# State of a chunked scan kept in the values tile, query products one half step earlier, and the last projections spread over more steps

## The chip, the cores and the metric

The kernel runs on one core of one Trainium2 chip. The metric is the device time of one execution in microseconds (us), the median over repeated runs; a profile of one execution shows when each engine worked. Engines are TensorE (PE in the profile), its weight load (PEld), VectorE (DVE), ScalarE (ACT), GpSimd (POOL) and SyncE (SP, which issues most transfers).

## The reference

One inference step of a two-layer hybrid encoder: 2048 new frames of one stream and 16 frames of each of 8 running streams, model width 1024. The first layer is a gated DeltaNet, the second an RWKV-7 time mixer with 16 heads of 64. The change is in the second layer only, whose recurrence is this (cut):

```
def mixer_b(h, x_prev, s0, mu, w_in, ...):
    ...
    rkvz = jnp.einsum('gbtd,dge->gbte', xs[:4], w_in.reshape(D, 4, W_B)).astype(f32)
    ...
    def step(S, inp):
        r_t, w_t, k_t, v_t, a_t, b_t = inp
        sa = jnp.einsum('bhvk,bhk->bhv', S, a_t)
        S = S * w_t[:, :, None, :] + sa[..., None] * b_t[:, :, None, :] + v_t[..., None] * k_t[:, :, None, :]
        return S, jnp.einsum('bhvk,bhk->bhv', S, r_t)
    ...
    S, o = lax.scan(step, s0.astype(f32), seq)
    ...
    y = o.astype(h.dtype) @ w_out
```

The final state S of the prompt stream is an output, and so are y and the states of the running streams.

## The kernel before

The first layer takes the first 2450 us. The second is done in six blocks of columns (frames): the first has two chunks of 64 frames and the running streams, the other five have six chunks each (384 columns). A block has eight head pairs q; a pair fills 128 partitions, 64 for each head. `b_steps` runs over the 48 combinations of block and pair as a pipeline of steps i. In step i the parts of several pairs run side by side: preparation of pair i, substitution of pair i-1 (`b_subst`: the triangular solve on VectorE, L842 and L844 in turn on the tiles sbt and TB, closed by the copy L847), inverse of pair i-2 (L1282 is its first product and reads T, which L1266 on GpSimd writes), scan of pair i-3 (`b_scan`), gate of pair i-4, output projection of two pairs every other step (L168, L169, L170), and the input projections of the next block (the stream `st`; L1060, L1061, L1062). A step has twelve rounds, and each part is a generator that is advanced a given number of times over the rounds.

The order in which this code emits matmuls is TensorE's order. The other engines' order is made by a list scheduler from due times, which come from the places of the consumers in TensorE's order.

A scan takes two half steps for each chunk c, usually one in each round. The tile XV[c] holds for each head the state in the head's own 64 partitions and the chunk's values in the others; R[q] holds the state of the pair in 128 partitions over all blocks. In the first half step TensorE forms px from XV[c] (L1380), ScalarE makes Sw, the state times the chunk's decay wc (L1382, from R), and then copies px over the state in XV[c] (L1383, L1384). In the second, TensorE forms the query product from R into po (L1387), pu from XV[c] (L1391) and the rest of po (L1396), and VectorE writes the next state twice: as two halves into XV[c+1] (L1393) and whole into R (L1394). po is one PSUM tile with one buffer; `b_centre` (L1455 to L1458, result OC) reads it when the scan is over. The gate (`b_gate`) turns OC on TensorE (L106), forms og in the tile bv (L1483, L1484) and splits it into oh (ScalarE) and ol (VectorE, L163) for the output projection; it also reads SZ, a kept projection result that comes by a transfer.

The projections come in units of six matmuls 128x384 (two for each of L1060, L1061, L1062), spread evenly over the rounds of a step: PACE = 17 units in a step, and LAST_PACE = 8 from step 40 on. At step 40 there are 57 units left.

Of the kernel before, what the change touches and what calls it, by code (L numbers as in the profile page):

```python
# [18 lines left out]
KT = 8  # L19
# [52 lines left out]
class _K:  # L72
# [856 lines left out]
    def b_steps(self, blocks, st):  # L929

        npair = len(blocks) * KT
        def at(i):
            return (blocks[i // KT], i % KT) if 0 <= i < npair else None
        self.b_load(*at(0))
        for i in range(npair + 6):
            parts = []
            if at(i):
                parts.append((self.b_prep(*at(i)), range(1, 13)))
            if at(i - 2):
                parts.append((self.b_inverse(*at(i - 2)), (1, 2, 3, 4, 5, 6, 7, 8, 10)))  # L940
            if at(i - 4):
                parts.append((self.b_gate(*at(i - 4)), (1, 2, 3, 6)))
            if at(i - 1):
                parts.append((self.b_subst(*at(i - 1)), range(1, 9)))
            if at(i - 3):
                b = at(i - 3)[0]
                parts.append((self.b_scan(*at(i - 3)), 2 * b["ncp"] + 6 * b["nsc"], 0.0, 1.0))
            j = i - 5
            if at(j) and j % 2 == 0:
                out = self.b_out(blocks[j // KT], (j % KT, j % KT + 1))  # L950
                if j < npair - 2:
                    parts.append((out, 8, 0.5, 1.0))
                else:
                    parts.append((chain(out, self.b_final(blocks[j // KT])), 21, 0.5, 1.0))
            if at(j) and j % KT == KT - 1 and j < npair - 1:
                parts.append((self.b_final(blocks[j // KT]), 13, 0.0, 1.0))
            m = PACE if i < npair - KT else LAST_PACE
            parts.append((islice(st, m), m, 0.0, 1.0))
            self.rounds(ROUNDS, parts)
            if at(i + 1):  # L960
                self.b_load(*at(i + 1))
        for p in range(KT):
            self.nc.sync.dma_start(self.io["o_pw"][p], self.R[p])
# [391 lines left out]
    def b_scan(self, b, q):  # L1355
# [16 lines left out]
                nc.sync.dma_start(SS[u], io["sw"][q][:, 4 * u:4 * u + 4])  # L1372
        for h in range(2):
            nc.gpsimd.tensor_copy(XV[HS[h], 0, h], self.R[q][HS[h]])
        for c in range(ncp):
            S = self.R[q]
            wc = wcs[:, c:c + 1]
            px = self.ps("r")
            for h in range(2):
                nc.tensor.matmul(px[HS[h], 0:64], lhsT=GM[:, c, h, 0:64], rhs=XV[:, c, h], start=True, stop=True, tile_position=(0, 64 * h))  # L1380
            Sw = self.mp.tile([P, 64], F32, name=self.nm("Sw"), tag="Sw", bufs=2)
            nc.scalar.activation(Sw, S, AF.Copy, scale=wc)  # L1382
            nc.scalar.copy(XV[HS[0], c, 0], px[HS[0], 0:64])  # L1383
            nc.scalar.copy(XV[HS[1], c, 1], px[HS[1], 0:64])  # L1384
            yield
            for h in range(2):
                nc.tensor.matmul(po[HS[1 - h], c * 64:(c + 1) * 64], lhsT=KR[HS[h], c, 1], rhs=S[HS[h]], start=True, stop=False,  # L1387
                                 tile_position=(64 * h, 64 - 64 * h))
            pu = self.ps("r")
            for h in range(2):  # L1390
                nc.tensor.matmul(pu[HS[h], 0:64], lhsT=TM[:, c, h], rhs=XV[:, c, h], start=True, stop=True, tile_position=(0, 64 * h))  # L1391
            for h in range(2 if c + 1 < ncp else 0):
                nc.vector.scalar_tensor_tensor(XV[HS[h], c + 1, h], pu[HS[h], 0:64], wc[HS[h]], Sw[HS[h]], op0=MUL, op1=ADD)  # L1393
            nc.vector.scalar_tensor_tensor(S, pu[:, 0:64], wc, Sw, op0=MUL, op1=ADD)  # L1394
            for h in range(2):
                nc.tensor.matmul(po[HS[1 - h], c * 64:(c + 1) * 64], lhsT=GM[:, c, h, 64:P], rhs=XV[:, c, h], start=False, stop=True, tile_position=(0, 64 - 64 * h))  # L1396
            yield
# [272 lines left out]
```

## Time and profile before

| | us |
|---|---|
| median of 3 runs (lowest, highest) | 4619.62 (4618.65, 4632.22) |
| the profiled execution's own time | 4624.97 |
| its span in the trace | 4623.2 |
| mean granted TensorE clock | 0.962 of full |
| busy: TensorE, VectorE, ScalarE, GpSimd | 4311.4, 3477.9, 2286.9, 1743.4 |

The span is what the trace covers from the first to the last instruction; 1.8 us of the execution's own time lie around it. Busy times are sums over the engine's instructions, so they say how full an engine is, and not which one ends a stage.

### The profile page before, as it was taken

What the parts mean: (1) busy time and instruction counts of PE and PEld (TensorE: products, weight loads), DVE (VectorE), ACT (ScalarE), POOL (GpSimd) and SP (SyncE); (2) the same over time, 40 slices, a digit from 0 to 9 for tenths busy, and PEclk for the clock granted to TensorE, in tenths of its full rate; (3) what the DMA queues carried; (4) which work ended last, traced back from release to release, by engine and by line L of the source; (5) the groups of instructions that cost most, each with busy time, mean ns of one, the idle gap of its engine ahead of it and who ended that gap; (6) DMA issues with size and microseconds to landing.
All of it is one profiled execution on the core that took longest, in us unless ns stands there. A gap on an engine that the chain in (4) does not pass through costs nothing. (4 is left out here: it accounts for less than half of the span.)

```text
span 4623.2 us, 104068 instructions
## 1 busy us (share of the span) xinstructions
PE 4311.4 (93%) x37093; PEld 3708.7 (80%) x37093; DVE 3477.9 (75%) x9203; ACT 2286.9 (49%) x6132; POOL 1743.4 (38%) x2507
## 2 busy tenths in 40 slices
PE   7999999999999999999987988999999999999996
PEld 6888788888888899999886767777878887887775
DVE  7888776676666766776677888877778778778874
ACT  5555454454344434434465565555555455445542
POOL 7666443322112211211204455545344434434441
PEclk9999999999999999999998989999999999999987
DMA  6666665556555676676555667756666665665542
GB/s 192 209 202 208 210 211 172 172 183 193 143 142 159 176 210 183 185 213 189 173 163 170 204 203 229 224 172 193 195 196 180 193 202 162 201 195 145 141 126 67
DMA packets 765670, 842.18 MB, mean 182 GB/s; under 512 B 263480, under 2 KB 497360, under 8 KB 765152
## 3 DMA queue, kind: packets, MB, share of 16 engines
q1 hardware_dynamic: 765152, 835.53, 60.2%
q8 instruction: 294, 4.82, 0.4%
q14 instruction: 224, 1.84, 0.1%
HBM read 632.73 MB, written 202.53 MB: 181 GB/s over the span
## 5 line engine op out<-in xcount | busy, mean ns | idle before, releaser
L451 PE MATMUL ps<-hh,whl 128*128 128x384 f32 (+1 forms) x1960 | 796.0, 406 | 10.7 <-ACT hh L162 9.4
L453 PE MATMUL ps<-hh,whl 128*128 128x384 f32 (+1 forms) x1960 | 712.5, 364 | 6.5 <-POOL whl L125 6.5
L452 PE MATMUL ps<-hl,whl 128*128 128x384 f32 (+1 forms) x1960 | 712.1, 363 | 1.7 <-DVE hl L163 1.5
L1060 PE MATMUL ps<-xh,whl 128*128 128x384 f32 (+1 forms) x1632 | 606.8, 372 | 33.6 <-ACT xh L162 20.4
L1061 PE MATMUL ps<-xl,whl 128*128 128x384 f32 (+1 forms) x1632 | 560.2, 343 | 18.3 <-POOL xl L163 8.9
L1062 PE MATMUL ps<-xh,whl 128*128 128x384 f32 (+1 forms) x1632 | 558.6, 342 | 8.6 <-DVE whl L125 8.3
L125 POOL TENSOR_TENSOR whl<-wraw,whl 128x256 fp32r<-128x256 f32 x454 | 374.3, 830 | 354.1 <-ACT whl L124 326.3
L571 DVE SCALAR_TENSOR_TENSOR cv<-pre,cw,cv 128x512 f32<-128x512 f32 (+3 forms) x576 | 376.4, 662 | 137.8 <-ACT cv L569 130.7
L451 PEld LDWEIGHTS ps<-hh,whl 128*128 128x128 f32 x1960 | 372.5, 190 | 63.0 <-issue 13.7
L168 PE MATMUL ps<-oh,whl 128*128 128x384 f32 (+2 forms) x1024 | 390.6, 381 | 26.7 <-DMA whl<-wd 14.2
L124 ACT CAST whl<-wraw 128x256 fp32r<-128x256 f32 x726 | 286.8, 402 | 250.8 <-DMA wraw<-in_w_b 70.6
L453 PEld LDWEIGHTS ps<-hh,whl 128*128 128x128 f32 x1960 | 371.9, 190 | 46.8 <-POOL whl L125 11.2
L452 PEld LDWEIGHTS ps<-hl,whl 128*128 128x128 f32 x1960 | 373.1, 190 | 34.6 <-DVE hl L163 5.2
L1060 PEld LDWEIGHTS ps<-xh,whl 128*128 128x128 f32 x1632 | 321.2, 197 | 76.5 <-ACT xh L162 26.5
L169 PE MATMUL ps<-ol,whl 128*128 128x384 f32 (+2 forms) x1024 | 367.2, 359 | 7.0 <-DVE ol L163 7.0
L842 DVE TENSOR_TENSOR sbt<-B,TB 48x15 f32<-48x15 f32 (+14 forms) x1320 | 350.0, 265 | 23.1 <-DMA B<-scr 2.3
L170 PE MATMUL ps<-oh,whl 128*128 128x384 f32 (+2 forms) x1024 | 364.6, 356 | 1.4 <-POOL whl L125 1.4
L844 DVE TENSOR_TENSOR TB<-TB,sbt 48x15 f32<-48x15 f32 (+14 forms) x1320 | 350.7, 266 | 19.8
L1061 PEld LDWEIGHTS ps<-xl,whl 128*128 128x128 f32 x1632 | 323.5, 198 | 30.0 <-DVE xl L163 15.5
L1062 PEld LDWEIGHTS ps<-xh,whl 128*128 128x128 f32 x1632 | 323.0, 198 | 16.0 <-DVE whl L125 15.3
L820 DVE TENSOR_TENSOR x<-x,ps 128x384 f32<-128x384 f32 (+1 forms) x320 | 191.0, 597 | 79.4 <-PE ps L170 79.1
L168 PEld LDWEIGHTS ps<-oh,whl 128*128 128x128 f32 x1024 | 197.6, 193 | 66.0 <-ACT oh L162 9.9
(349 smaller groups left out, 10249.7 us busy)
## 6 DMA issues: line engine op xcount, KB each, us to landing
whl<-wd SPq DMA_DIRECT2D x1582, 256.0 KB
wd<-whl SPq DMA_DIRECT2D x428, 256.0 KB
wraw<-in_w_a SPq DMA_DIRECT2D x288, 128.0 KB
wraw<-in_w_b SPq DMA_DIRECT2D x256, 128.0 KB
kvd<-kvo SPq DMA_DIRECT2D x160, 192.0 KB
xn<-x1d SPq DMA_DIRECT2D x80, 192.0 KB
wraw<-in_w_ao SPq DMA_DIRECT2D x96, 128.0 KB
xn<-in_x SPq DMA_DIRECT2D x32, 256.0 KB
```

Of the source, the lines that this page charges most:

```text
L125: (self.nc.gpsimd if tag == "o" else self.weng).tensor_tensor(w[:, 1], raw, w[:, 0].bitcast(F32), op=SUB)
L168: self.nc.tensor.matmul(out, lhsT=wh, rhs=hh, start=first and i == 0, stop=False)
L169: self.nc.tensor.matmul(out, lhsT=wh, rhs=hl, start=False, stop=False)
L170: self.nc.tensor.matmul(out, lhsT=wl, rhs=hh, start=False, stop=i == n - 1)
L451: nc.tensor.matmul(p, lhsT=wh[:, k % 2], rhs=hh, start=k == 0, stop=False)
L452: nc.tensor.matmul(p, lhsT=wh[:, k % 2], rhs=hl, start=False, stop=False)
L453: nc.tensor.matmul(p, lhsT=wl[:, k % 2], rhs=hh, start=False, stop=k == KT - 1)
L571: nc.vector.scalar_tensor_tensor(o, f(j), self.cw[:, ct, j:j + 1], o, op0=MUL, op1=ADD)
L844: nc.vector.tensor_tensor(T[:, j + 1:16, 0:j + 1], T[:, j + 1:16, 0:j + 1], o, op=SUB)
L1060: nc.tensor.matmul(o, lhsT=wh[:, i], rhs=xh, start=k == 0, stop=False)
L1061: nc.tensor.matmul(o, lhsT=wh[:, i], rhs=xl, start=False, stop=False)
L1062: nc.tensor.matmul(o, lhsT=wl[:, i], rhs=xh, start=False, stop=k == KT - 1)
```

## The change

There are three edits. First, in all chunks but a scan's last VectorE writes the new state only into XV[c+1]; R[q] is written once, after the last chunk, where it carries the state to the next block and to the output. ScalarE's Sw is therefore made from the two state halves in XV[c], as two operations on 64 partitions, ahead of the copies of px that overwrite them. Second, the query product reads the state from XV[c], and stands in the first half step ahead of px. Third, in the last four steps of the 48 and after them the pace of projections is 4 units a step in place of 8.

```
@@ b_steps
-            m = PACE if i < npair - KT else LAST_PACE
+            m = PACE if i < npair - KT else LAST_PACE if i < npair - 4 else LAST_PACE // 2
@@ b_scan
         for c in range(ncp):
-            S = self.R[q]
             wc = wcs[:, c:c + 1]
+            for h in range(2):
+                nc.tensor.matmul(po[HS[1 - h], c * 64:(c + 1) * 64], lhsT=KR[HS[h], c, 1], rhs=XV[HS[h], c, h], start=True, stop=False,
+                                 tile_position=(64 * h, 64 - 64 * h))
             px = self.ps("r")
...
-            nc.scalar.activation(Sw, S, AF.Copy, scale=wc)
-            nc.scalar.copy(XV[HS[0], c, 0], px[HS[0], 0:64])
-            nc.scalar.copy(XV[HS[1], c, 1], px[HS[1], 0:64])
+            for h in range(2):
+                nc.scalar.activation(Sw[HS[h]], XV[HS[h], c, h], AF.Copy, scale=wc[HS[h]])
+            for h in range(2):
+                nc.scalar.copy(XV[HS[h], c, h], px[HS[h], 0:64])
             yield
-            for h in range(2):
-                nc.tensor.matmul(po[HS[1 - h], c * 64:(c + 1) * 64], lhsT=KR[HS[h], c, 1], rhs=S[HS[h]], start=True, stop=False,
-                                 tile_position=(64 * h, 64 - 64 * h))
             pu = self.ps("r")
...
-            for h in range(2 if c + 1 < ncp else 0):
-                nc.vector.scalar_tensor_tensor(XV[HS[h], c + 1, h], pu[HS[h], 0:64], wc[HS[h]], Sw[HS[h]], op0=MUL, op1=ADD)
-            nc.vector.scalar_tensor_tensor(S, pu[:, 0:64], wc, Sw, op0=MUL, op1=ADD)
+            if c + 1 < ncp:
+                for h in range(2):
+                    nc.vector.scalar_tensor_tensor(XV[HS[h], c + 1, h], pu[HS[h], 0:64], wc[HS[h]], Sw[HS[h]], op0=MUL, op1=ADD)
+            else:
+                nc.vector.scalar_tensor_tensor(self.R[q], pu[:, 0:64], wc, Sw, op0=MUL, op1=ADD)
```

In the changed code the lines have other numbers: L1387 becomes L1379, L1380 becomes L1383, L1391 becomes L1392, L1396 becomes L1399, the writes of XV and R become L1395 and L1397, Sw L1386 and the copies L1388, the centre L1458 to L1461, and the gate's two products L1486 and L1487. The 57 units left at step 40 went out as eight in each of steps 40 to 46 and one in step 47; now steps 40 to 43 have eight each, steps 44 to 49 four each and step 50 one. There are 256 chunks in 48 scans, so R was written 256 times and is written 48 times; Sw took 256 operations on ScalarE and takes 512. The number of matmuls is the same.

TensorE, one chunk of a scan in step 21, before (matmuls of other parts stand between the two half steps; ps_44548 is po, the other ps are px and pu):

```order
L1380 MATMUL ps_44809<-XV_43904,GM_42912 64x64 x2
...
L106 MATMUL ps_44848<-ident,OC_44448 64x64 x12
L1387 MATMUL ps_44548<-R_30368,KR_42575 64x64 x2
L1391 MATMUL ps_44875<-XV_43904,TM_43903 64x64 x2
L1396 MATMUL ps_44548<-XV_43904,GM_42912 64x64 x2
```

The same chunk now (po is ps_44566):

```order
L1379 MATMUL ps_44566<-XV_43924,KR_42590 64x64 x2
L1383 MATMUL ps_44829<-XV_43924,GM_42927 64x64 x2
...
L106 MATMUL ps_44869<-ident,OC_44466 64x64 x12
L1392 MATMUL ps_44894<-XV_43924,TM_43923 64x64 x2
L1399 MATMUL ps_44566<-XV_43924,GM_42927 64x64 x2
```

The query product moved from the start of the second half step to the start of the first, and reads XV.

VectorE, behind that same chunk's second half step, before (m is a small tile of the preparation, xt and xl belong to the inputs of the projections):

```order
L1191 TENSOR_SCALAR m_11116_44784<-m_11116_44784 128x6
L842 TENSOR_TENSOR sbt_44684<-B_44437,TB_44539 48x60
L1483 SCALAR_TENSOR_TENSOR bv_42031<-ps_44848,hp,bv_42031 128x384
L1393 SCALAR_TENSOR_TENSOR XV_43904<-ps_44875,wc_42560,Sw_44812 64x64 x2
L1484 SCALAR_TENSOR_TENSOR bv_42031<-bv_42031,hp,SZ_44531 128x384
L1394 SCALAR_TENSOR_TENSOR R_30368<-ps_44875,wc_42560,Sw_44812 128x64
L844 TENSOR_TENSOR TB_44539<-TB_44539,sbt_44684 48x10x6
L163 TENSOR_TENSOR xl_44720<-xt_44716,xh_44719 128x384
L163 TENSOR_TENSOR ol_44864<-bv_42031,oh_44863 128x384
```

And now:

```order
L844 TENSOR_TENSOR TB_44557<-TB_44557,sbt_44699 48x11x5
L163 TENSOR_TENSOR xl_44741<-xt_44737,xh_44740 128x384
L1395 SCALAR_TENSOR_TENSOR XV_43924<-ps_44894,wc_42575,Sw_44832 64x64 x2
L1486 SCALAR_TENSOR_TENSOR bv_42045<-ps_44869,hp,bv_42045 128x384
L842 TENSOR_TENSOR sbt_44702<-B_44457,TB_44557 48x60
L1487 SCALAR_TENSOR_TENSOR bv_42045<-bv_42045,hp,SZ_44549 128x384
L844 TENSOR_TENSOR TB_44557<-TB_44557,sbt_44702 48x10x6
```

The write of R is gone, and XV's pair moved ahead of the gate's first product and of one substitution operation.

VectorE, the end of the last substitution in step 48, before:

```order
L844 TENSOR_TENSOR TB_62224<-TB_62224,sbt_62415 48x4x12
L842 TENSOR_TENSOR sbt_62428<-B_62162,TB_62224 48x39
L844 TENSOR_TENSOR TB_62224<-TB_62224,sbt_62428 48x3x13
L1394 SCALAR_TENSOR_TENSOR R_30374<-ps_62521,wc_60675,Sw_62515 128x64
L842 TENSOR_TENSOR sbt_62431<-B_62162,TB_62224 48x28
L1455 TENSOR_REDUCE gn_62527<-ps_62233 128x6
L844 TENSOR_TENSOR TB_62224<-TB_62224,sbt_62431 48x2x14
L1456 TENSOR_SCALAR gn_62527<-gn_62527 128x6
L842 TENSOR_TENSOR sbt_62462<-B_62162,TB_62224 48x15
L1458 TENSOR_TENSOR OC_62528<-ps_62233,gn_62527 128x384
L844 TENSOR_TENSOR TB_62224<-TB_62224,sbt_62462 48x15
L847 COPY TB_62224<-TB_62224 48x256
```

And now:

```order
L844 TENSOR_TENSOR TB_62190<-TB_62190,sbt_62397 48x4x12
L842 TENSOR_TENSOR sbt_62417<-B_62117,TB_62190 48x39
L844 TENSOR_TENSOR TB_62190<-TB_62190,sbt_62417 48x3x13
L842 TENSOR_TENSOR sbt_62420<-B_62117,TB_62190 48x28
L844 TENSOR_TENSOR TB_62190<-TB_62190,sbt_62420 48x2x14
L842 TENSOR_TENSOR sbt_62454<-B_62117,TB_62190 48x15
L844 TENSOR_TENSOR TB_62190<-TB_62190,sbt_62454 48x15
L847 COPY TB_62190<-TB_62190 48x256
L1395 SCALAR_TENSOR_TENSOR XV_61680<-ps_62502,wc_60667,Sw_62476 64x64 x2
L1397 SCALAR_TENSOR_TENSOR R_30374<-ps_62519,wc_60667,Sw_62514 128x64
L1458 TENSOR_REDUCE gn_62525<-ps_62199 128x6
```

The scan's last two writes and the centre moved behind the substitution's closing copy; earlier in the same substitution a kept value's product (L1086) came in, since projection units now run in this step.

## Rows read from the trace of the kernel before

**Rows 1.** The page's first part: busy time of each engine, share of the span, instructions

```profile
PE 4311.4 (93%) x37093; PEld 3708.7 (80%) x37093; DVE 3477.9 (75%) x9203; ACT 2286.9 (49%) x6132; POOL 1743.4 (38%) x2507
```

**Rows 2.** Table of stretches: window, length, busy by engine (instructions), granted clock, DMA

```profile
2759.70:4169.60 1409.90, 1316.14 (x15421) 1120.41 (x15420) 1116.97 (x2929) 746.32 (x2021) 636.02 (x778) 0.96 0.66 195
...
4367.80:4402.90 35.10, 33.19 (x445) 27.58 (x444) 29.41 (x81) 18.56 (x54) 18.99 (x20) 0.85 0.47 132
4402.90:4445.10 42.20, 37.48 (x475) 31.97 (x475) 34.59 (x89) 15.56 (x47) 18.92 (x27) 0.92 0.69 209
4445.10:4476.60 31.50, 30.47 (x429) 25.05 (x428) 23.70 (x73) 15.14 (x46) 14.38 (x17) 0.84 0.32 86
4476.60:4513.00 36.40, 31.83 (x433) 25.11 (x432) 30.11 (x81) 14.82 (x46) 18.30 (x25) 0.91 0.34 87
4513.00:4536.90 23.90, 13.80 (x327) 11.32 (x326) 15.76 (x61) 11.49 (x38) 7.48 (x10) 0.88 0.17 35
4536.90:4562.20 25.30, 22.92 (x338) 18.96 (x338) 9.72 (x24) 9.70 (x33) 1.52 (x2) 0.78 0.17 51
```

**Rows 3.** Timeline of step 21: start, us, engine, line [idle before it]

```profile
3373.44 0.34 PE L1060 MATMUL ps<-xh,whl 128*128 128x384 f32 x1
...
3373.62 0.34 PE L1061 MATMUL ps<-xl,whl 128*128 128x384 f32 x1
...
3376.05 0.21 DVE L842 TENSOR_TENSOR sbt<-B,TB 48x60 f32<-48x60 f32 x1
3376.19 0.60 DVE L1483 SCALAR_TENSOR_TENSOR bv<-ps,hp,bv 128x384 f32<-128x384 f32 x1
3376.72 0.59 DVE L1393 SCALAR_TENSOR_TENSOR XV<-ps,wc,Sw 64x64 f32<-64x64 f32 x2
...
3377.04 0.72 PE L1380 MATMUL ps<-XV,GM 128*64 128x64 f32 x4 [2.26 <-DVE XV L1393]
...
3378.50 0.53 PE L170 MATMUL ps<-oh,whl 128*128 128x384 f32 x1
...
3378.82 0.53 PE L168 MATMUL ps<-oh,whl 128*128 128x384 f32 x1
```

**Rows 4.** Waits of TensorE, 2545 to 4300: us in total, times, longest

```profile
PE ps L1380 <- DVE XV L1393: 34.5, 24, 2.6
...
PE ps L169 <- DVE ol L163: 5.9, 14, 0.7
```

**Rows 5.** Tile Sw: ns min/median/max; then who waited for it (us, times)

```profile
L1382 ACT ACTIVATE Sw<-R,wc x256: 330/348/368, 2461.0 to 4580.5; 128x64 f32<-128x64 f32 x128
L1394 DVE SCALAR_TENSOR_TENSOR R<-ps,wc,Sw x256: 231/283/286, 2549.8 to 4581.1; 128x64 f32<-128x64 f32 x128
...
  ACT Sw L1382: 145.0, 96
...
  PE ps L1380: 43.3, 38
```

**Rows 6.** Timeline of VectorE around one write of R

```profile
3366.82 0.28 DVE L1394 SCALAR_TENSOR_TENSOR R<-ps,wc,Sw 128x64 f32<-128x64 f32 x1
3367.02 0.77 DVE L842 TENSOR_TENSOR sbt<-B,TB 48x28 f32<-48x28 f32 x1
```

**Rows 7.** Timeline of the bare chain of step 50, the query product

```profile
4577.69 0.48 PE L1387 MATMUL ps<-R,KR 64*64 64x64 f32 x4
```

**Rows 8.** Timeline of the first block, L1380 ahead of the previous scan's centre

```profile
2890.03 0.34 PE L1380 MATMUL ps<-XV,GM 128*64 128x64 f32 x4
...
2891.28 0.28 DVE L1458 TENSOR_TENSOR OC<-ps,gn 128x128 f32<-128x128 f32 x1
```

**Rows 9.** Timeline of ScalarE, two L1382 back to back

```profile
4562.04 0.59 ACT L1382 ACTIVATE Sw<-R,wc 128x64 f32<-128x64 f32 x2 [0.45 <-DVE R L1394]
```

**Rows 10.** Timeline of step 48: the last substitution's copy and the product behind it

```profile
4531.50 0.38 DVE L847 COPY TB<-TB 48x256 f32<-48x256 f32 x1
...
4536.86 1.44 PE L1282 MATMUL ps<-T,N 64*64 64x64 f32 x22 [7.22 <-POOL T L1266]
```

## The prediction, made before the changed kernel ran

> **What bounds the kernel now.** I read the page's busy line first, then the table of stretches, the waits of TensorE, the tile views, and last the timeline of single steps.
>
> TensorE is busy 93% of the span [rows 1], so only its idle time, the time at half speed and the order at the end can give anything. In the steady stretch of layer 2, 2759.70 to 4169.60, TensorE works 1316.14 of 1409.90 us: 93.8 us idle. [...]
>
> The largest item in TensorE's waits is the one that the change touches: L1380, the first product of a scan chunk, waits 34.5 us in 24 waits for XV, VectorE's state of the chunk before (L1393) [rows 4]. In the whole layer it is 43.3 us in 38 waits [rows 5]. The longest shows why: at 3377.04 TensorE had idled 2.26 us, and XV had started at 3376.72 only because VectorE did a substitution operation at 3376.05 and the gate's L1483 at 3376.19 first [rows 3]. The reader is to see a queue on VectorE, not a slow operation.
>
> **The change, part by part.**
>
> *State written once.* 256 writes of R become 48: 208 fewer. One lasts 283 ns [rows 5]; what it holds on VectorE is less: it starts at 3366.82 and the next operation at 3367.02 [rows 6], a slot of 0.20 us. So 208 x 0.20 = 41.6 us of VectorE go, nearly all of it off the path. Behind the second XV write, which starts at partition 64, the next operation now stands where R stood. [...] I take 0.20.
>
> What does that give on TensorE? R(c) stands behind XV(c) and before XV(c+1), so if VectorE's queue is full all the way, the next XV comes one slot earlier: 38 x 0.20 = -7.6 us. Where the queue runs dry in between it gives nothing; the bounds are 0 and -7.6, or with longer queues removed, the whole 43.3.
>
> *Order on VectorE.* Without R the scheduler puts XV ahead of the gate's first product in steps such as step 21: 0.53 us for that product (3376.19 to 3376.72) and 0.14 us for the substitution operation (3376.05 to 3376.19) [rows 3], 0.67 us, at nine such places -6.0. The gate's values come later by XV's pair in turn; behind them wait the output products: L169 already waits 5.9 us in 14 waits for ol [rows 4]. I give half back, +3. In the steps between, XV stands behind one or two more substitution operations, 0.2 to 0.45 us; against their R slot that costs about +2.5 over the layer. Term for the scan: -7.6 - 6.0 + 3.0 + 2.5 = -8.
>
> *Fewer pauses, less half speed.* If the time at half speed falls in proportion to the idle time, 8/93.8 of 50 us: -4.5. Bounds: 0 (each pause that is left is enough to lower the clock) and -10.
>
> *Other waits for VectorE* (casts, rests, kept values) shrink with its load: -2, between 0 and -5.
>
> *Query products in the first half step.* The same matmuls, moved: L1387 becomes L1379, ahead of px, and reads XV instead of R. Before px it costs its own time, 0.48 us at the lower clock on the bare chain [rows 7], of which the part for the second half of XV lies in the wait for it; behind px twelve projection matmuls (2.1 us) usually cover ScalarE's copies, so nothing in the steady steps. It also opens po one round sooner, so it must wait until the previous scan's centre (L1458) has read po. In the six-chunk steps the centre is done by then. Not in the short first block: L1380 at 2890.03 stands 1.5 us ahead of the centre's end (2891.28 + 0.28) [rows 8]; two of its eight steps are like that: +2.6, between 0 and +8 if all were.
>
> *Sw from XV.* One operation of 348 ns [rows 5] becomes two on 64 partitions. Two such operations back to back take 0.59 us [rows 9], so +0.24 us for each of 256 chunks, 61 us of ScalarE. It must now run ahead of the px copies, which overwrite its input. It is hidden as long as TensorE is busy with the query product and px for as long (0.6 us); ScalarE also no longer waits for R, where it idled 145.0 us in 96 waits [rows 5]. I cost it at nothing; bare, it is up to 0.24 a chunk.
>
> *Pace of the last block.* Twelve projection units (six matmuls each: 1.05 us at full clock, 1.9 at half; about 1.2 at the clock there) leave steps 44 to 46 (four each) and go to 47 (three), 48 (four), 49 (four) and 50 (one). Steps 44 to 46 last 35.10, 42.20 and 31.50 us with 33.19, 37.48 and 30.47 of TensorE and 29.41, 34.59 and 23.70 of VectorE [rows 2]. Four units are 4.8 us; VectorE lets the first two shrink less: -3.5, -3, -4. Step 47 idles 4.6 us, so three units cost about +1.5. Step 48 idles 10.1 of 23.90, of it 7.22 waiting for T at 4536.86, the end of a chain through the last substitution on VectorE, whose closing copy starts at 4531.50 [rows 2, 10]. The four units there are free, and the chain gets shorter: six R slots less (1.2), one XV pair and the centre moved behind it (1.8), one kept value's product more (0.5), about -2 in sum. Step 49 has 22.92 busy of 25.30 [rows 2], so four units show: +3. Step 50: one unit +1.2, and L1379 on the bare chain 5 x 0.26: +1.3. Sum: -10.5 + 1.5 - 2 + 3 + 2.5 = -5.5; bounds -12 and +5 (nothing gained in 44 to 46 because VectorE's chain sets them).
>
> **Sum.** -8 - 4.5 - 2 + 2.6 - 5.5 = -17.4 us, from the profiled run's 4624.97 to 4607.6. That run lay 5.4 us above the median of the three, 4619.62, so I say 4603 (-0.36%). A measurement of this kernel tells about 0.3%, 13.9 us, from no change.
>
> **Rivals.**
>
> *Given back (same).* The waits do not vanish but change their names: XV comes sooner, og, oh and ol later, and TensorE stops at L168 or L169 two matmuls further on. For it: at 3377.04 the output product follows px directly, and VectorE stays nearly as full (79% to 77%). Against it: ol's waits are at most 0.7 us. Scan -2, no clock gain, tail -3, first block +2.6: -2 to -8, 4612 to 4618.
>
> *Slower: ScalarE's pair on the chain.* Where XV is late, the pair starts only when XV is there, and the copies of px wait 0.59 us behind it instead of running first; then pu (L1392) and the next XV come later, and the lateness adds up over the six chunks of a scan. [...] No row has the two halves; the back-to-back row gives 0.24 for the second operation [rows 9]. At 0.24 exposed in every chunk it is +61 - 17 = +44: 4647; it decides from 17.4/0.24 = 73 of 256 chunks. Against it: ScalarE is at 53%, and no wait of TensorE for the px copies stands among the larger ones.
>
> *Not what it says.* What waited for R was ScalarE's Sw [rows 5], which TensorE did not wait for; if VectorE's queue before each late XV is made of long products alone, the removed slot never counts. Then only tail and order act: -10, 4610.
>
> **How the numbers follow.** Forecast, gain of 0.3% or somewhat more: 0.50, its own range 4592 to 4608. Given back or not what it says: 0.38, 4608 to 4622. Slower chain, or a tail in which 49 and 50 cost more than 44 to 46 give: 0.12, of it 0.08 beyond 0.3%. The boundary at 4605.8 cuts the forecast's range near its upper end; a gain larger than the sum, if the clock gives more, lies on the same side. Faster 0.54, same 0.37, slower 0.09. Range: 4585 (scan -16, clock -8, tail -12) to 4628.
>
> **What the profile after would show.** L1379 and L1383 together wait less than 43.3 us for XV, by about 8; R is written 48 times and ScalarE's idle time before Sw falls below 145.0; at step 21's place XV starts before the gate's product and the wait is under 1.6 us. Granted clock in the steady stretch at 0.96 or 0.97. Steps 44 to 46 shorter by about 10 us, the wait for T in step 48 under 3, step 49 longer by 3. I am wrong if the waits at L168 and L169 grow by as much as those for XV shrink, if TensorE now waits at L1392 for the px copies, or if steps 44 to 46 keep their length.

## The result, and the profile after

The changed kernel took 4667.88 us (median of 4 runs, 4661.74 to 4680.08) against 4619.14 (4614.15 to 4632.22) for the kernel before: a ratio of 1.0102, with a 95% interval of 1.0085 to 1.012. I had forecast 4603 and a gain. The profiled execution took 4662.48 us; its span is 4660.8, at a mean granted clock of 0.958. The two profiled executions lie 37.5 us apart and the medians 48.7, so the traces below explain the smaller of the two.

The busy line of the page after, to be read beside [rows 1]:

```profile
PE 4334.0 (93%) x37093; PEld 3729.6 (80%) x37093; DVE 3436.6 (74%) x8995; ACT 2383.5 (51%) x6388; POOL 1733.4 (37%) x2507
```

The counts moved as foreseen: 208 operations fewer on VectorE, 256 more on ScalarE, the same matmuls. VectorE works 41.3 us less, and TensorE, with the same instructions, 22.6 us more; in steps 8 to 40, as read below, 153.6 us ran at half clock, where it had been 109.2.

The table of stretches after: the steady stretch, then steps 44 to 48, each beside its row in [rows 2].

```profile
2763.30:4204.90 1441.60, 1339.63 (x15420) 1140.60 (x15419) 1091.23 (x2780) 811.79 (x2194) 622.54 (x778) 0.95 0.64 191
4401.00:4434.40 33.40, 28.78 (x422) 23.80 (x421) 26.60 (x73) 20.97 (x60) 16.51 (x20) 0.80 0.36 103
4434.40:4475.90 41.50, 35.23 (x452) 28.84 (x451) 33.71 (x86) 17.09 (x51) 20.88 (x27) 0.88 0.61 172
4475.90:4503.20 27.30, 24.08 (x405) 19.81 (x404) 23.11 (x67) 17.32 (x52) 12.24 (x15) 0.94 0.37 100
4503.20:4545.50 42.30, 33.87 (x453) 27.77 (x451) 26.24 (x76) 16.66 (x50) 18.78 (x27) 0.88 0.36 88
4545.50:4572.00 26.50, 19.26 (x351) 15.66 (x350) 15.44 (x56) 14.39 (x46) 7.50 (x10) 0.98 0.33 93
```

The loss is in the steady stretch. With its edges at the first L1121 of step 8 and of step 40 in each kernel, the difference of the two spans (37.6 us) divides so: steps 8 to 40 +30.1, steps 40 to 46 -7.0, step 47 to the end +11.0, steps 0 to 8 -1.9. The first layer, whose code is the same, gave +5.5; its end lay anywhere from 2452 to 2474 us in the profiles of this study, so it is left out of all that follows.

The same stretch, steps 8 to 40, first of before and then of after:

```profile
2759.74:4226.64 1466.90, 1366.39 (x15947) 1161.80 (x15947) 1166.68 (x3047) 783.37 (x2112) 661.54 (x809) 0.96 0.65 193
```

```profile
2763.28:4260.24 1496.96, 1389.01 (x15948) 1181.44 (x15947) 1139.85 (x2894) 851.84 (x2292) 649.39 (x809) 0.95 0.64 189
```

TensorE's idle time (length less its busy time) went from 100.5 to 107.9, +7.4 us. The trace's clock records, in which the clock stands at full or at half, put 109.2 us of this stretch at half before, in 22 pieces, and 153.6 us in 30 pieces after. In step 21 of before one projection matmul starts 0.18 us after another at full clock (3373.44 to 3373.62) and 0.32 us at half (3378.50 to 3378.82) [rows 3]. So half speed loses 0.14 of 0.32, about 45%, and the 44.4 us more cost about 20, an estimate. So idle time and half speed make about 27 of the 30.1 us, by an account of one execution each.

The wait that the change was to shorten, in the view of tile Sw of the kernel after (its fellow is [rows 5]):

```profile
L1386 ACT ACTIVATE Sw<-XV,wc x512: 327/344/359, 2466.5 to 4617.2; 64x64 f32<-64x64 f32 x171
...
L1397 DVE SCALAR_TENSOR_TENSOR R<-ps,wc,Sw x48: 262/282/286, 2558.6 to 4619.2; 128x64 f32<-128x64 f32 x48
...
  ACT Sw L1386: 108.7, 69
  PE ps L1379: 46.3, 36
```

TensorE waits 46.3 us in 36 waits for XV, where it was 43.3 in 38. ScalarE's wait ahead of Sw did fall, from 145.0 to 108.7, and TensorE's wait did not follow.

What VectorE waited for in steps 8 to 40, first before, then after:

```profile
DVE XV L1393 <- PE ps L1391: 45.4, 38, 2.1
...
DVE xl L163 <- ACT xh L162: 6.6, 18, 0.4
DVE bv L1483 <- PE ps L106: 5.8, 8, 0.9
```

```profile
DVE XV L1395 <- PE ps L1392: 66.9, 50, 2.0
...
DVE bv L1486 <- PE ps L106: 14.8, 12, 2.3
DVE xl L163 <- ACT xh L162: 13.8, 18, 1.7
```

VectorE was relieved of 26.8 us there (1166.68 to 1139.85) and now waits 37.7 us more in these three lines, 21.5 of it for pu from TensorE. Over all lines it idles 56.9 us more, which is the 26.8 and the 30.1 by which the stretch grew: the time came back as waiting.

Step 21, the example of [rows 3], in the timeline after:

```profile
3386.68 0.54 DVE L163 TENSOR_TENSOR xl<-xt,xh 128x384 fp32r<-128x384 f32 x1
...
3387.15 0.59 DVE L1395 SCALAR_TENSOR_TENSOR XV<-ps,wc,Sw 64x64 f32<-64x64 f32 x2
...
3387.47 0.65 PE L1379 MATMUL ps<-XV,KR 64*64 64x64 f32 x4 [2.18 <-DVE XV L1395]
3387.65 0.71 ACT L1386 ACTIVATE Sw<-XV,wc 64x64 f32<-64x64 f32 x2
3387.78 0.62 DVE L1486 SCALAR_TENSOR_TENSOR bv<-ps,hp,bv 128x384 f32<-128x384 f32 x1
```

XV does stand ahead of the gate's product now, as the order had shown. But the rest of a projection input, xl, stands ahead of XV with 0.47 us to the next start, and TensorE waits 2.18 us where it waited 2.26.

### The profile page after: what moved, and what is told of

The parts are those of the page before. It is cut to its first block, busy times and chain, and to the rows that moved or that the text cites. A ratio compares the mean times of both kernels' runs of the same rounds, so it can differ in the third digit from the quotient of the medians.

```text
span 4660.8 us, 104241 instructions
## 1 busy us (share of the span) xinstructions
PE 4334.0 (93%) x37093; PEld 3729.6 (80%) x37093; DVE 3436.6 (74%) x8995; ACT 2383.5 (51%) x6388; POOL 1733.4 (37%) x2507
## 5 line engine op out<-in xcount | busy, mean ns | idle before, releaser
L451 PE MATMUL ps<-hh,whl 128*128 128x384 f32 (+1 forms) x1960 | 799.0, 408 | 11.5 <-ACT hh L162 10.1
L1061 PE MATMUL ps<-xl,whl 128*128 128x384 f32 (+1 forms) x1632 | 561.1, 344 | 20.0 <-POOL xl L163 11.9
L168 PE MATMUL ps<-oh,whl 128*128 128x384 f32 (+2 forms) x1024 | 390.0, 381 | 25.5 <-DMA whl<-wd 15.0
L169 PE MATMUL ps<-ol,whl 128*128 128x384 f32 (+2 forms) x1024 | 366.0, 357 | 5.4 <-DVE ol L163 5.1
L844 DVE TENSOR_TENSOR TB<-TB,sbt 48x15 f32<-48x15 f32 (+14 forms) x1320 | 340.0, 258 | 21.6
L1061 PEld LDWEIGHTS ps<-xl,whl 128*128 128x128 f32 x1632 | 324.9, 199 | 31.8 <-POOL xl L163 16.3
L168 PEld LDWEIGHTS ps<-oh,whl 128*128 128x128 f32 x1024 | 197.3, 193 | 63.5 <-ACT oh L162 8.3
```

The source lines that it names most:

```text
L168: self.nc.tensor.matmul(out, lhsT=wh, rhs=hh, start=first and i == 0, stop=False)
L169: self.nc.tensor.matmul(out, lhsT=wh, rhs=hl, start=False, stop=False)
L451: nc.tensor.matmul(p, lhsT=wh[:, k % 2], rhs=hh, start=k == 0, stop=False)
L844: nc.vector.tensor_tensor(T[:, j + 1:16, 0:j + 1], T[:, j + 1:16, 0:j + 1], o, op=SUB)
L1061: nc.tensor.matmul(o, lhsT=wh[:, i], rhs=xl, start=False, stop=False)
```

## The experiments

Each ratio is to the kernel before on the same chip, with its 95% interval. "Half speed" and "idle" are TensorE's in steps 8 to 40 of the profiled execution, as above (before: 109.2 and 100.5 us).

| run | ratio | interval | length of steps 8 to 40 | half speed | idle |
|---|---|---|---|---|---|
| e1_pace | 1.0026 | 1.0011 to 1.004 | 1465.30 | 99.0 | 102.2 |
| e2_scan | 1.0083 | 1.0061 to 1.0105 | 1504.66 | 148.8 | 116.8 |
| e3_query | 1.0067 | 1.0045 to 1.0088 | 1489.71 | 139.9 | 109.0 |
| e4_sw | 1.0058 | 1.0039 to 1.0076 | 1478.50 | 115.0 | 101.5 |
| e5_px_first | 1.0042 | 1.0026 to 1.0058 | 1485.48 | 105.8 | 99.9 |
| e6_lead7 | 1.0041 | 1.0027 to 1.0054 | 1489.99 | 143.4 | 112.1 |
| e7_pace46 | 1.0003 | 0.9989 to 1.0018 | 1472.73 | 112.6 | 104.2 |
| e9_scan_lead5 | 1.0088 | 1.0067 to 1.011 | 1501.44 | 160.4 | 111.1 |
| e10_query_order | 1.006 | 1.0041 to 1.0079 | 1492.05 | 143.4 | 110.4 |
| e11_scan_order | 1.0174 | 1.0153 to 1.0195 | 1525.51 | 163.8 | 128.6 |
| e12_order_only | 1.0043 | 1.0027 to 1.0058 | 1481.23 | 92.2 | 116.9 |
| e13_query_twice | 1.0065 | 1.0045 to 1.0085 | 1489.40 | 95.6 | 96.8 |
| e14_scan_twice | 1.012 | 1.01 to 1.014 | 1504.06 | 119.5 | 101.6 |
| e15_sw_order | 1.0165 | 1.0138 to 1.0191 | 1530.56 | 177.5 | 129.8 |
| e16_pu_first | 1.0018 | 1.0001 to 1.0036 | 1478.61 | 99.0 | 100.8 |
| e17_pu_order | 1.0017 | 1.0001 to 1.0033 | 1482.89 | 105.8 | 98.8 |

The lengths are of one execution and move by a few us between kernels that share the code of this stretch (before, e1_pace, e7_pace46: 1465.30 to 1472.73), so I lean on the ratios, and on the lengths only for differences well above that.

### The edits one by one

e1_pace is before with the pace edit alone. e2_scan is after with before's pace. e3_query is before with the query product moved alone (R is still written in every chunk, and Sw still made from it). e4_sw is e3_query with Sw made from XV.

```diff
e1_pace (to before)
-            m = PACE if i < npair - KT else LAST_PACE
+            m = PACE if i < npair - KT else LAST_PACE if i < npair - 4 else LAST_PACE // 2
e3_query (to before; the two lines leave the second half step)
+            for h in range(2):
+                nc.tensor.matmul(po[HS[1 - h], c * 64:(c + 1) * 64], lhsT=KR[HS[h], c, 1], rhs=XV[HS[h], c, h], start=True, stop=False, ...)
             px = self.ps("r")
e4_sw (to e3_query)
-            nc.scalar.activation(Sw, self.R[q], AF.Copy, scale=wc)
+            for h in range(2):
+                nc.scalar.activation(Sw[HS[h]], XV[HS[h], c, h], AF.Copy, scale=wc[HS[h]])
```

> Only the pace of projections in the last steps is changed; the scan is that of before. Theory 'order' (the loss is made in the steady steps, by the new order on VectorE): about 4619 to 4626, since in the two traces the stretch from step 40 to the end grew by only some 4 us (250.0 + 146.6 before, 243.0 + 157.6 after). Theory 'pace' (the units moved into the last steps lengthen the end): 4650 or more.

> The whole edit of the scan with the pace of before. Theory 'order', and also theories 'pair' and 'query': 4655 to 4670, nearly all of the loss. Theory 'pace': 4605 to 4620.

> Only the query product is moved into the first half step, where it reads the state from XV; R is written in every chunk and Sw comes from R as before. Theory 'query' (the product ahead of px lengthens the chain from chunk to chunk, and waits for po): 4645 or more. Theories 'order' and 'pair': 4612 to 4628.

> As the run before, and Sw is made from the two halves in XV by two operations of ScalarE; R is still written in every chunk. Theory 'pair' (two operations ahead of the px copies make the copies late): 4645 or more, with the waits of TensorE's L1392 for the copies above the 4.4 us of the changed kernel's trace. Theory 'order' (the loss comes with the removal of R's writes): 4612 to 4632.

Measured: 4637.38 against 4630.0 us (e1_pace), then 4668.96, 4659.46 and 4657.68. The pace costs 0.26%, which lies between the two theories. The whole scan edit costs 0.83%, and the edit that I had priced at nothing, the query product's move, costs 0.67% alone, in the order that the scheduler makes for it. e4_sw is as slow as theory 'pair' had it, but so is e3_query without the pair, and TensorE's waits for px's copies (L1392) are 2.2 us in e4_sw, below the 4.4 named there: the pair shows no cost in these two. From e4_sw to e2_scan (R written once) there is no gain but a loss: all four runs of e2_scan (4662.32 to 4675.81) lie above all four of e4_sw (4652.35 to 4661.72), with 11 us between the medians.

### Is it the place, or the order that it brings about?

e5_px_first puts the query product behind px in the same half step. e6_lead7 is before with the list scheduler's lead at 7 in place of 6 in the second layer: the same work, another order. e7_pace46 is before's scan with another pace. e9_scan_lead5 is e2_scan with a lead of 5.

```diff
e5_px_first (to e3_query)
-            <query product>
             px = self.ps("r")
             <px>
+            <query product>
e6_lead7 (to before; e9_scan_lead5: the same with 5, to e2_scan)
+    two = next(j for j, e in enumerate(log) if any(o[0].startswith("R_") for o in e[2]))
-        d -= LEAD_DMA if dma else LEAD
+        d -= LEAD_DMA if dma else LEAD if j < two else 7
e7_pace46 (to before)
+            m = PACE if i < npair - KT else LAST_PACE // 2 if npair - 4 <= i < npair - 2 else LAST_PACE
```

> As the run with the query product alone moved (ratio 1.0067), but inside the first half step it stands behind px instead of ahead of it; R is written in every chunk and Sw comes from R. Theory 'ahead of px' (the product delays px, and with it the copies and the next state): ratio 0.998 to 1.002. Rival 'out of the second half step' (the product covered part of VectorE's time between pu and the next px, wherever in the first half step it stands now): 1.004 to 1.008, with the same waits for XV of about 1.5 us in the even steps.

> The kernel before with no work changed: in the second layer the scheduler's lead is 7 places instead of 6, which puts products for TensorE (xt, xl, T) behind one more substitution operation on VectorE in about as many places as the whole edit of the scan does. Theory 'order' (that shift of order alone costs time): ratio 1.003 or more. Rival (order is neutral, work and chain decide): 0.998 to 1.002.

> The scan of before; the pace is 4 units in steps 44 and 45 only and 8 again from step 46. Theory 'cover' (the units taken out of step 46 hid the chain to T, which then let TensorE wait 6.57 us at the start of step 47): the wait falls under 3 us and the ratio is 0.997 to 1.001. Rival (units late in the pipeline lengthen the end by themselves): 1.002 to 1.004, with a wait at the start of step 47 or not.

> The whole edit of the scan with the pace of before (ratio 1.0083), and a lead of 5 places in the second layer, which brings xt and xl on VectorE on average back to their places among the substitution operations. Theory 'order' (what the removal of R's writes costs is the order that the scheduler makes without them): 1.003 to 1.006. Rival (the chain itself got longer): 1.007 to 1.010.

Measured: 4648.74 against 4632.32 (e5_px_first), 4647.73, 4631.51 and 4669.72. e5_px_first lies in the range of its rival, though not by longer waits: in the whole layer TensorE waits 42.5 us for XV there, and 43.3 before. Order matters: a change of the lead alone costs 0.41%, half as much as the whole scan edit. So the experiments up to here could not tell the product's place from the order that the scheduler made of it, and another lead did not win back what the scan edit lost.

e7_pace46 settles the tail. It spares units in steps 44 and 45 and lets eight go again from step 46, and comes out level with before. The product that reads T at the start of step 47, in before, e1_pace, after and e7_pace46:

```profile
4477.03 0.92 PE L1282 MATMUL ps<-T,N 64*64 64x64 f32 x24
```

```profile
4487.08 1.54 PE L1282 MATMUL ps<-T,N 64*64 64x64 f32 x24 [6.57 <-POOL T L1266]
```

```profile
4510.26 1.23 PE L1282 MATMUL ps<-T,N 64*64 64x64 f32 x18 [6.58 <-POOL T L1266]
```

```profile
4489.92 0.91 PE L1282 MATMUL ps<-T,N 64*64 64x64 f32 x24
```

Before, the eight units of step 46 hid the chain to T. With four, the chain stands bare for 6.6 us at the start of step 47; with eight again the wait is gone.

### The order held fixed

In these three VectorE, GpSimd and SyncE are held to a recorded order, by ordering edges that add no wait between engines. e10_query_order is e3_query with those and ScalarE in before's order; e11_scan_order is e2_scan in before's order, ScalarE free since its instructions differ; e12_order_only is before's work in e2_scan's order, in which R's 208 further writes have no place and go where the scheduler puts them. No run holds before to its own order, so what the edges cost by themselves is not shown directly. e3_query and e10_query_order, and below e16_pu_first and e17_pu_order, are the same work without and with them, and differ by 0.07% and 0.01%.

```diff
+    for e, ks in order.items():
+        prev = None
+        for k in ks:
+            for inst in made.get(k, []):
+                if prev is not None:
+                    tc.add_manual_dep(inst, prev.name, info, reason="order")
+                prev = inst
```

> As the run with the query product alone moved (ratio 1.0067), but VectorE, ScalarE, GpSimd and SyncE are held to the order in which they run in the kernel before, by ordering edges; only TensorE's order differs from before. Theory 'order' (moving the product costs because the scheduler answers with another order on the other engines): ratio 0.998 to 1.002. Theory 'place' (the product ahead of px costs by itself): 1.005 to 1.008.

> The whole edit of the scan with the pace of before (ratio 1.0083), with VectorE, GpSimd and SyncE held to their order in the kernel before, R's 208 writes left out; ScalarE's order stays the scheduler's. Theory 'order': 0.996 to 1.002, since only the gain of the removed slots is left. Theory 'place': 1.004 to 1.008, what the query product costs.

> The reverse: the scan and pace of before with all its work, R's writes too, but VectorE, GpSimd and SyncE held to the order that the scheduler makes for the whole edit of the scan. Theory 'order': 1.004 to 1.010, the loss without the edit. Theory 'place': 0.998 to 1.002.

Measured: 4660.55 against 4631.03 us (e10_query_order), 4711.07 and 4649.81. With every other engine in before's order the moved product still costs 0.60%, so most of e3_query's loss is the place itself. The order that the scan edit brings about costs 0.43% with before's work; TensorE idles 16.4 us more there, and 17.0 us less run at half speed. And before's order does not suit the changed scan: 1.74%, twice what it loses in the order that the scheduler makes for it, and more than either theory gave. So place and order do not simply add up; e15_sw_order, below, shows with which edit that comes.

The steady stretch of e10_query_order:

```profile
2772.98:4265.03 1492.05, 1381.65 (x15947) 1176.05 (x15947) 1165.12 (x3047) 783.31 (x2112) 661.34 (x809) 0.95 0.65 190
```

Beside before's row: +25.1 us, of it +9.9 idle and +15.3 busy. The 34.2 us more at half speed, at 45%, are 15.4, as much as the busy part. e6_lead7, with the product in its old place and the same 143.4 us at half speed, is busy 11.5 us longer than before, so half speed makes some 11 to 15 of the 15.3. In the whole layer TensorE waits 52.6 us for XV in 39 waits, where it was 43.3 in 38.

Of the 25.1 us 21.2 arise in the even steps. TensorE in step 24 of before, from its first L1121 on: a query product alone ahead of pu (L1391), the wait in the middle of the step, and late in the step a query product among the inverse's last products (L1343, L1346).

```profile
3501.50 0.51 PE L1121 MATMUL ps<-LT,w 128*128 128x384 f32 x2
...
3511.68 0.33 PE L1387 MATMUL ps<-R,KR 64*64 64x64 f32 x4
3511.94 0.34 PE L1391 MATMUL ps<-XV,TM 128*64 128x64 f32 x4
...
3516.01 0.65 PE L1380 MATMUL ps<-XV,GM 128*64 128x64 f32 x4 [1.03 <-DVE XV L1393]
3516.59 0.44 PE L1060 MATMUL ps<-xh,whl 128*128 128x384 f32 x1
3516.86 0.33 PE L1061 MATMUL ps<-xl,whl 128*128 128x384 f32 x1
3517.04 0.34 PE L1062 MATMUL ps<-xh,whl 128*128 128x384 f32 x1
...
3524.24 0.33 PE L1343 MATMUL ps<-GM,T 64*64 64x64 f32 x4
...
3524.99 0.22 PE L1343 MATMUL ps<-GM,T 64*64 64x64 f32 x2
3525.00 0.27 PE L1387 MATMUL ps<-R,KR 64*64 64x64 f32 x2
...
3525.32 0.34 PE L1391 MATMUL ps<-XV,TM 128*64 128x64 f32 x4
```

The same in e10_query_order, whose L1122, L1283, L1383, L1387, L1061 to L1063, L1344 and L1397 are the step's first line, the inverse's first product, the query product, px, the projections, the inverse's last products and pu:

```profile
3524.25 0.51 PE L1122 MATMUL ps<-LT,w 128*128 128x384 f32 x2
...
3525.22 0.27 PE L1383 MATMUL ps<-XV,KR 64*64 64x64 f32 x2
3525.27 0.28 PE L1283 MATMUL ps<-T,N 64*64 64x64 f32 x3
...
3538.87 0.80 PE L1383 MATMUL ps<-XV,KR 64*64 64x64 f32 x4 [1.65 <-DVE XV L1400]
3539.60 0.48 PE L1387 MATMUL ps<-XV,GM 128*64 128x64 f32 x4
3540.01 0.69 PE L1061 MATMUL ps<-xh,whl 128*128 128x384 f32 x1
3540.49 0.52 PE L1062 MATMUL ps<-xl,whl 128*128 128x384 f32 x1
3540.82 0.52 PE L1063 MATMUL ps<-xh,whl 128*128 128x384 f32 x1
...
3550.16 0.33 PE L1344 MATMUL ps<-GM,T 64*64 64x64 f32 x4
...
3551.24 0.34 PE L1397 MATMUL ps<-XV,TM 128*64 128x64 f32 x4
```

A query product among other 64x64 products takes no time that shows: the inverse's last products take 1.08 us up to pu with it (3524.24 to 3525.32) and 1.08 us without it (3550.16 to 3551.24). Alone it takes 0.26 us up to pu (3511.68 to 3511.94). Before, the free places are late in the step; now they are early, beside the inverse's first products. So, counted from the step's first line, TensorE comes to the wait in the middle 0.5 us sooner (13.48 us before, 12.97 now), and XV lets it go on 0.1 us later (14.51 and 14.62). It waits 1.65 us in place of 1.03, and comes out at the lower clock: a projection matmul lasts 0.52 us, where it was 0.33. Step 24 is 3.4 us longer.

Steps 26, 32 and 34 are 2.5 to 2.6 us longer, and not all in the same way. The wait in the middle is 1.20, 1.16 and 1.19 us there, where it was 0.94, 1.18 and 0.95; behind the first the projection matmuls last 0.34 us, behind the other two 0.52. So the earlier arrival is shown in step 24, and only argued for the rest.

That the wait's length decides the clock is more than the rows bear out. Step 32, first of before and then of e10_query_order:

```profile
3877.83 0.65 PE L1380 MATMUL ps<-XV,GM 128*64 128x64 f32 x4 [1.18 <-DVE XV L1393]
...
3878.69 0.33 PE L1061 MATMUL ps<-xl,whl 128*128 128x384 f32 x1
```

```profile
3910.22 0.65 PE L1383 MATMUL ps<-XV,KR 64*64 64x64 f32 x4 [1.16 <-DVE XV L1400]
...
3911.64 0.52 PE L1062 MATMUL ps<-xl,whl 128*128 128x384 f32 x1
```

Behind as long a wait TensorE ran at full speed in the one and at half speed in the other. And in step 21 the half clock began 0.4 us behind a wait of 2.26 us before (3377.48 in the clock records), and 2.5 us behind one of 2.18 us after (3389.94).

### Giving the time back

If TensorE loses by getting to that wait too soon, the same work added again at the old place should win the clock back. e13_query_twice does that to e10_query_order, e14_scan_twice to e2_scan: a second query product of the same size, into a free part of pu's tile, which nothing reads. e15_sw_order is e4_sw in before's order (VectorE, GpSimd, SyncE).

```diff
e13_query_twice (to e10_query_order; e14_scan_twice: the same from XV, to e2_scan)
+            for h in range(2):
+                nc.tensor.matmul(pu[HS[1 - h], 64:P], lhsT=KR[HS[h], c, 1], rhs=self.R[q][HS[h]], start=True, stop=True, ...)
             <pu>
```

> As e10 (the query product in the first half step, the other engines in the order of before, ratio 1.0060), and a second product of the same size stands where the query product stood before; its result goes to unused columns of pu's bank and is read by nobody. Theory 'pause' (TensorE, relieved in the second half step, comes earlier to a state that VectorE delivers no sooner; the longer pause brings the clock down): the added 256 products make the kernel faster, 1.000 to 1.004, and the time at half speed in the steady steps falls from e10's 143 us to 95 to 125. Rival 'ahead of px': 1.006 to 1.014, the loss stays and the added work comes on top.

> The whole edit of the scan with the pace of before (ratio 1.0083), and the same second product at the query product's old place, reading XV; its result is read by nobody, and the order of the other engines is the scheduler's. Theory 'pause': 1.002 to 1.007. Rival 'ahead of px': 1.008 to 1.016.

> Query product moved, Sw by two operations from XV, R still written in every chunk, with VectorE, GpSimd and SyncE held to the order of before and ScalarE free: e11 (1.0174) with R's writes put back. If the missing writes make e11 slow (a fixed order in which XV comes a slot sooner and waits for its inputs): 1.004 to 1.009. If ScalarE's pair under a fixed order does: 1.014 to 1.020.

Measured: 4661.76 against 4634.44 us (e13_query_twice), 4690.44 and 4709.98. The steady stretch of e13_query_twice:

```profile
2773.70:4263.10 1489.40, 1392.63 (x16668) 1182.93 (x16667) 1159.01 (x3043) 784.55 (x2112) 661.27 (x809) 0.97 0.66 190
```

Idle time and half speed did return below before's, 96.8 and 95.6 us, as the theory of the pause says, and so did the waits for XV in the whole layer (39.3 us). The time did not return, against what I had expected: 1.0065 and 1.012 lie in the ranges of the rival. TensorE's busy time rose by 11.0 us although 47.8 us less ran at half speed (21.5 us at 45%): the added products cost about 32 us, an estimate from these two rows, and that eats the gain. It agrees with a count: about 120 of the 180 added products stand alone, at 0.26 us each. So a shorter pause seems to be worth something here, and filling it with work costs more.

e15_sw_order stands at 1.0165, as e11_scan_order at 1.0174. With the order held, writing R once therefore changes nothing that these runs show; what separates both from e10_query_order (1.0060) is ScalarE's pair, and ScalarE's freedom to set its own order. With the scheduler's order the pair cost nothing (e3_query to e4_sw). TensorE's waits for px's copies are 2.7 and 2.3 us in these two and 2.3 in e10_query_order, so it is not these that grew.

### The other direction

If reaching the wait sooner loses, pu could be sent sooner instead, so that VectorE has XV earlier. e16_pu_first has in the second half step pu, then the rest of po, then the query product; e17_pu_order is the same with the other engines in before's order.

```diff
e16_pu_first (to before)
-            <query product into po, start=True, stop=False>
             <pu>
+            <rest of po, start=True, stop=False>
+            <query product into po, start=False, stop=True>
```

> The kernel before, with the query product behind pu and the rest of po in the second half step, so that pu, and with it the next state, comes a quarter of a microsecond sooner; the other engines in the scheduler's order. Theory 'pause' (the less TensorE has to wait for the state, the less half speed): 0.996 to 1.001 if the order is as good as that of before, and up to 1.004 if the scheduler's new order costs what it cost elsewhere. Rival (any other place of the product costs): 1.004 or more.

> The same with VectorE, ScalarE, GpSimd and SyncE held to their order in the kernel before. Theory 'pause': 0.995 to 0.999, the waits for XV below 40 us in the whole layer. Rival (any other place of the product costs): 1.003 or more.

Measured: 4641.81 against 4631.76 us and 4640.47, +0.18 and +0.17%: no gain, and less than the rival's 0.3 to 0.4%. TensorE's waits for XV in the whole layer are 44.8 and 41.8 us, where I had expected under 40 of the second. Idle time and half speed are before's, but TensorE's busy time in steps 8 to 40 is 1377.84 and 1384.11 us against 1366.39, 11 to 18 us more. e5_px_first shows the same more plainly:

```profile
2761.77:4247.25 1485.48, 1385.55 (x15947) 1176.04 (x15947) 1161.17 (x3042) 786.75 (x2112) 659.40 (x809) 0.96 0.65 191
```

Its idle time (99.9) and half speed (105.8) are before's too, and it is busy 19.2 us longer with the same matmuls. Before, 61 of the 180 query products of the prompt's chunks in these steps stand among other 64x64 products; in e5_px_first, e16_pu_first and e17_pu_order none does. At the 0.26 us that one takes alone that is 16 us, an estimate, and the three are busy 11 to 19 us longer. In e10_query_order and after it is 53 and 56 of 180, so little of their loss is of this kind. No run of this study beat the kernel before.

## Why the prediction was wrong, by its own steps

**The query products, the step that failed first.** "The same matmuls, moved ... so nothing in the steady steps." Measured: +0.60% with the order held (e10_query_order). I priced the product where it went and not where it left. Nearly as many run free beside products of their shape as before (53 of 180 for 61), but early in the step and not late, and in step 24 TensorE then reaches the wait for XV sooner while XV is no earlier. In the sum its waits for XV are 52.6 us for 43.3, and 34.2 us more of the steady stretch run at half speed. What I counted as hidden was work that had kept TensorE from a wait.

**State written once.** The count (208), the slot (26.8 us less VectorE time for 153 fewer rows of the steady stretch, 0.175 each; forecast 0.20) and the order at step 21 were right. The conclusion, -7.6 us for a shorter queue, was not: XV's waits are 46.3 us in place of 43.3, e15_sw_order to e11_scan_order shows no gain, and e4_sw to e2_scan, where the scheduler makes a new order, a loss of 11 us. With the order held nothing came of it, which is the bound that I gave for a queue that runs dry in between. In after VectorE waits 66.9 us for pu where it waited 45.4, so its write of XV is late also because TensorE's product comes late, and not only because its own queue is long.

**Order on VectorE.** -6.0 for XV ahead of the gate's product rested on one change per step. The scheduler moved other things ahead of XV as well (xl in step 21, whose wait I had put under 1.6 us and which is 2.18). e12_order_only measures the whole order with before's work: +0.43%, where my terms for it (-6.0, +3.0 and +2.5) made -0.5 us. Waits for ol (L169) moved little, 0.7 us longest before and 1.3 after, so the rival "given back" is not what happened either.

**Fewer pauses, less half speed.** The 50 us from which this term starts are shown by no run; the clock records of before put 99.0 us of that stretch at half clock, which at 45% is about 45, an estimate. -4.5 became about +20 us, at a granted clock of 0.95 where I had 0.96 or 0.97. I had scaled half speed with the idle time; it went up by two fifths while the idle time rose by 7%.

**Other waits for VectorE.** -2 became about +7: TensorE's waits for VectorE in lines other than those for XV, 2545 to 4300, are 49.1 us where they were 41.7.

**ScalarE's pair.** I took +0.24 us for each chunk from two whole operations back to back [rows 9]. Measured: ScalarE is busy 96.6 us longer, 0.38 for each of 256 chunks, and 138 of the 256 pairs last 0.69 to 0.73 us. As "nothing" in the sum it held in the scheduler's order: TensorE waits for px's copies (L1392 for XV) only 4.4 us in 11 waits. The rival that was to lose by it named the right sign for the wrong reason. Its 4647 also takes the gain of 17 off twice: 4619.6 + 44 is 4664, and that this comes near the measured time is luck, since the pair shows no cost of its own in the scheduler's order.

**The wait for po.** +2.6 in the first block does not show: steps 0 to 8 are 1.9 us shorter, and no wait for the centre stands among TensorE's waits there.

**The tail.** -5.5 became +4.0 in after, and e1_pace alone costs 0.26%. Steps 44 to 46 did shrink (108.8 to 102.2 us, forecast -10.5), and step 48's wait fell from 7.22 to 4.86 us (forecast under 3). The missing term is step 47: I gave it +1.5 for its three units and did not ask what the eight of step 46 covered. They covered T: the product that reads it waits 6.58 us at the start of step 47 in after, and did not wait before. Step 48 grew by 2.6 where I had -2, and the rest behind it by 2.5 (forecast +5.5).

**Signs and slips.** None of the three signs that I had named for being wrong came: the waits at L168 and L169 for the gate's values did not grow (10.9 us in all before, 9.0 after), those at L1392 are 4.4 us, and steps 44 to 46 got shorter. They watched places that were not the ones that failed. Two slips decided nothing: the sum gives 4602.2 and not 4603; and the wait of 2.26 us is not the longest of its line, which is 2.6 [rows 4].

Four things stay open. Why the pair costs about 1% when the other engines are held to before's order. Which places make up the 0.43% of the new order. Where, outside step 24, the moved product's waits arise. And what sets the clock behind a wait: in e12_order_only the idle time rose from 100.5 to 116.9 us and the half speed fell from 109.2 to 92.2.

## What to carry to other kernels

A product that moves is priced twice: where it arrives, and where it leaves, with the products of its shape that it ran beside and the wait that it kept its engine from (e10_query_order: +0.60%, waits for XV 52.6 us for 43.3). Where two engines take turns waiting for each other, freeing one need not shorten the turn (26.8 us less work on VectorE in steps 8 to 40, and a stretch 30.1 us longer); look at which waits the freed engine has itself before counting its slots as gain. Work that looks like it crowds a step can be the cover of a chain that ends behind it (the 6.6 us for T at the start of step 47): before it is spread, look for the first wait after it and what fed that.

## What the runs showed of the hardware

Query products of 64x64 among other 64x64 products took no time that shows: the inverse's last products took 1.08 us with one among them and 1.08 us without. Alone ahead of 128-row products one took 0.26 us, and kernels in which all stand alone are busy 11 to 19 us longer in steps 8 to 40 for the same matmuls. Two ScalarE operations on the two halves of the partitions (344 ns each) last 0.69 to 0.73 us in 138 of the 256 pairs of after and 0.57 to 0.59 in 71, and the other 47 are spread from 0.62 to 4.61, some with other work between; two on all 128 partitions lasted 0.59 [rows 9]. And a kernel with the same work in another order, by one unit of a scheduler's lead, had 143.4 us at half clock in the steady stretch where it had 109.2, in one execution each.
